# Emission order in place of the scheduler's on VectorE, ScalarE and GpSimd, in a loop of seven products per weight block

## The chip, the cores and the metric

The kernel runs on one core of one Trainium2 chip. The metric is the device time of one execution in microseconds, the median of several runs. Before the change it is 1908.83 us (three runs, 1908.06 to 1911.45).

## What is computed

The reference is a decoder trunk of two layers on 512 tokens of width 1024, all in float32. Each layer has two half-step SwiGLU blocks around a mixer (a gated short convolution in layer 0, differential attention in layer 1). Cut to the part that matters here, a SwiGLU block is

```python
def swiglu(x, w_gu, w_down):
    gate, up = jnp.split(x @ w_gu, 2, axis=-1)
    return (jax.nn.silu(gate) * up) @ w_down

h = h + 0.5 * rmsnorm(swiglu(rmsnorm(h, g[0]), ffn_w_gu[l, 0], ffn_w_down[l, 0]), g[1])
```

with 2816 hidden columns, and it runs four times: twice in each layer.

## The kernel before

**Precision.** Every float32 operand of a product is split into a high part `hi` (ScalarE writes it rounded to the matmul's float32r) and the rest `lo` (the operand minus `hi`, on VectorE or GpSimd). A product of two operands is three matmuls: hi by hi, hi by lo, lo by hi.

**The gate and up projection.** `ffn` works through 22 blocks `f` of 128 hidden columns. For the first four (`PLAIN`) function `job` multiplies directly. For the other 18, function `seven` treats the block as a 2 by 2 matrix of pieces (gate or up, by first or second half of the 1024 inputs: a11, a12, a21, a22) against a 2 by 2 matrix of token pieces (input half by left or right 256 tokens), and computes it with seven products of pieces instead of eight. The left factors are a11, a12, a22 themselves and four sums: s2 = a21 + a22 - a11, s1 = a21 + a22, s3 = a11 - a21, s4 = a12 - s2. The right factors are made once per FFN (`RightFactors`).

Each product is 12 matmuls of 128 by 128 by 256 columns (four tiles along the inputs, three matmuls each; function `product`, L336). They accumulate in three PSUM tiles a, b and c. The order of the products on TensorE, in the source, is: a11 into a, s2 into b, s1 into c, s3 into b, a12 into a, s4 into c, a22 into b. Between them the results are read out while the accumulation goes on:

- after a11, ScalarE copies a into u1 (L613); after s2, VectorE adds b and u1 to u2 (L598, `after6`)
- after s3, `after7`: VectorE makes u3 = b + u1 (L601) and, from it, su = c + u3 (L602)
- after a12, ScalarE takes the Silu of a (L617)
- after s4, `after3`: VectorE makes g2 = c + u2 (L605), and ScalarE its Silu (L606)
- after a22, `after4`: VectorE makes the last quarter su = b + u1 (L609), and GpSimd multiplies gate by up into `praw` (L611).

Since s4 goes on accumulating in c, its first matmul must wait until L602 has read c.

**The weights.** Class `Sum` makes the left factors of a later block while TensorE works on this one. There are eight buffers `wf`; when a product is closed, its buffer is free and the next factor in line is made, that of the product eight places later. A plain factor takes a ScalarE copy (L206) and a GpSimd subtraction (L207). A sum is formed in a PSUM tile `sums` by VectorE (L214 and L215 for s2 with s1 in passing, L221 for s3, L225 for s4), then ScalarE writes `hi` (L227), and VectorE writes `lo` (L229). That last step is held back in the source (`Sum.pending`, `flush`) until the next factor is made, so that VectorE does not sit waiting for ScalarE. L214 and L221 have two operands in SBUF, and the GpSimd operations L207 and L611 as well.

**What sets the order.** Nothing in the kernel orders the engines' queues by hand, apart from one short block at the start. Each engine runs its queue strictly in order, and a scheduler in the framework decides at build time what stands where. Two loads of 1 MB raw weights (`raw`, SyncE's queue) are in flight or in use at a time.

After the 22 blocks, `down` multiplies by the down projection (L384), again split in three matmuls.

Of the kernel before, what the change touches and what calls it, by code (L numbers as in the profile page):

```python
# [12 lines left out]
I32 = mybir.dt.int32  # L13
AF = mybir.ActivationFunctionType
ALU = mybir.AluOpType
PSUM = bass.MemoryType.PSUM
DRAM = bass.MemoryType.DRAM

# [5 lines left out]
NF = 2816 // P  # L24
# [8 lines left out]
PLAIN = 4  # L33
# [80 lines left out]
def trunk(ctx, tc, x, gu, dn, norm_g, cin, ck, cout, kvg, wk, wv, wq, lamp, subg, wo, out):  # L114
# [7 lines left out]
    work = ctx.enter_context(tc.tile_pool(name="work", bufs=1))  # L122
    psum = ctx.enter_context(tc.tile_pool(name="psum", bufs=1, space=PSUM))
    dram = ctx.enter_context(tc.tile_pool(name="dram", bufs=1, space=DRAM))
# [3 lines left out]
    def acc_tile(name):  # L128
        return psum.tile([P, 2, 512], F32, tag="acc", bufs=3, name=name)
# [30 lines left out]
    class Unit:  # L160
# [6 lines left out]
        def make(self):  # L167
# [5 lines left out]
            else:  # L173
# [5 lines left out]
                for a, (hi, lo) in enumerate(self.halves):  # L179
                    nc.vector.tensor_tensor(lo, raw[:, a * 512:(a + 1) * 512], hi.bitcast(F32), ALU.subtract)  # L180
            if self.u:
# [5 lines left out]
    class Sum:  # L187
# [10 lines left out]
        def make(self):  # L198
# [6 lines left out]
            if plain is not None:  # L205
                nc.scalar.activation(hi, plain, AF.Copy)  # L206
                nc.gpsimd.tensor_tensor(lo, plain, hi.bitcast(F32), ALU.subtract)  # L207
                Sum.flush()
            else:
# [3 lines left out]
                if self.form == "s2":  # L213
                    nc.vector.tensor_tensor(s0, a21, a22, ALU.add)  # L214
                    nc.vector.tensor_tensor(s1, s0, a11, ALU.subtract)  # L215
                    src = s1
                elif self.form == "s1":
                    src = s0
                elif self.form == "s3":
                    Sum.flush()  # L220
                    nc.vector.tensor_tensor(s0, a11, a21, ALU.subtract)  # L221
                    src = s0
                else:
                    Sum.flush()
                    nc.vector.tensor_tensor(s1, a12, s1, ALU.subtract)  # L225
                    src = s1
# [86 lines left out]
    def proj(o, key, u, xk, cols, ks=range(KT)):  # L313

        w = weights.get(key, u)
        n = cols.stop - cols.start
        for k in ks:
            hi, lo = w[k // 4]
            c = slice(k % 4 * P, (k % 4 + 1) * P)
            xh, xl = xk(k)  # L320
            for a, b in ((hi, xh), (hi, xl), (lo, xh)):
                nc.tensor.matmul(o[:, cols], a[:, c], b[:, cols],  # L322
                                 start=(k == 0 and b is xh and a is hi), stop=(k == KT - 1 and a is lo))
            later.tick(3 * 0.21 * n / 512)

    def close(*key):
        weights.done(*key)

    def product(o, key, xk, first, last):

        hi, lo = weights.get(*key)[0]
        for k in range(4):
            c = slice(k * P, (k + 1) * P)
            xh, xl = xk(k)
            for a, b in ((hi, xh), (hi, xl), (lo, xh)):
                nc.tensor.matmul(o, a[:, c], b, start=(first and k == 0 and b is xh and a is hi),  # L336
                                 stop=(last and k == 3 and a is lo), skip_group_check=True)
            later.tick(3 * 0.21 * 256 / 512)

    def two_then_two(nf, tail, stag):  # L340

        seq = [(f, t) for f in range(nf - tail) for t in range(NT)]
        for g in ((0, 1), (2, 3)):
            seq += [(f, t) for f in range(nf - tail, nf - stag) for t in g]
            for t in g:
                seq += [(f, t) for f in range(nf - stag, nf)] + [(None, t)]
        return seq
# [82 lines left out]
    def bcast(row, tag):  # L430
        g = work.tile([P, D], F32, tag=tag, bufs=1, name=tag)
        nc.sync.dma_start(g, row.partition_broadcast(P))
        return g
# [59 lines left out]
    def xk_of(xT):  # L493
        return lambda k: (xT[0][:, k, :], xT[1][:, k, :])

    def raw_blocks(pool):

        blocks = {}

        def place(f):  # L500
            if f // KT not in blocks:
                blocks[f // KT] = pool.tile([P, KT, S], F32, tag="praw", bufs=3, name="praw")
            return blocks[f // KT][:, f % KT, :]
        return place

    def raw_parts(pool, praws):
        def parts(f, toks):
            a, n = toks[0] * P, len(toks) * P
            ps = pool.tile([P, 2, S], F32R, tag="pair", bufs=3, name="psp")
            split(ps[:, 0, :n], ps[:, 1, :n], praws[f][:, a:a + n])  # L510

            def at(t):
                c = slice(t * P - a, (t + 1) * P - a)
                return ps[:, 0, c], ps[:, 1, c]
            return at
        return parts
# [44 lines left out]
    def ffn(pool, l, i, xT, finish, halves=True, right=None):  # L561
        key = f"{l}{i}"
        praws = [None] * NF
        place = raw_blocks(pool)
        tiles = {}

        def job(f, cols):
            if f not in tiles:
                tiles[f] = acc_tile("gu")
            ps = tiles[f]  # L570
            for s in range(2):
                proj(ps[:, s, :], "gu" + key, 2 * f + s, xk_of(xT), cols)
                if cols.stop == S:
                    close("gu" + key, 2 * f + s)
            if cols.stop == S:
                sil = pool.tile([P, 2, S], F32, tag="pair", bufs=3, name="sil")[:, 0, :]
                nc.scalar.activation(sil, ps[:, 0, :], AF.Silu)
                praws[f] = place(f)
                nc.vector.tensor_tensor(praws[f], sil, ps[:, 1, :], ALU.mult)

        def seven(f, e):

            if e == 0:
                tiles["abc"] = [acc_tile(n) for n in "abc"]
            a, b, c = (t[:, e, LEFT] for t in tiles["abc"])
            tmp = work.tile([P, 4, 256], F32, tag="tmp", bufs=2, name="u")
            u1, u2, u3, g2 = (tmp[:, n, :] for n in range(4))
            su = pool.tile([P, 2, S], F32, tag="pair", bufs=3, name="su")

            def step(o, form, factor, first, last, then):  # L590
                product(o, ("gu" + key, f, form), right.t[factor], first, last)
                then()
                if f == NF - 1 and factor in right.slots:
                    right.done(factor)
                close("gu" + key, f, form)

            def after6():
                nc.vector.tensor_tensor(u2, b, u1, ALU.add)  # L598

            def after7():  # L600
                nc.vector.tensor_tensor(u3, b, u1, ALU.add)  # L601
                nc.vector.tensor_tensor(su[:, 1, RIGHT], c, u3, ALU.add)  # L602

            def after3():
                nc.vector.tensor_tensor(g2, c, u2, ALU.add)  # L605
                nc.scalar.activation(su[:, 0, RIGHT], g2, AF.Silu)  # L606

            def after4():
                nc.vector.tensor_tensor(su[:, 1, LEFT], b, u1, ALU.add)  # L609
                praws[f] = place(f)  # L610
                nc.gpsimd.tensor_tensor(praws[f], su[:, 0, :], su[:, 1, :], ALU.mult)  # L611

            step(a, "a11", "b11", True, True, lambda: nc.scalar.activation(u1, a, AF.Copy))  # L613
            step(b, "s2", "t2", True, True, after6)
            step(c, "s1", "t1", True, True, lambda: None)
            step(b, "s3", "t3", False, True, after7)
            step(a, "a12", "b21", False, True, lambda: nc.scalar.activation(su[:, 0, LEFT], a, AF.Silu))  # L617
            step(c, "s4", "b22", False, True, after3)
            step(b, "a22", "t4", False, True, after4)

        if halves:
            later.keep(2)
            for f in range(3):
                job(f, FIRST)
            later.keep(0)
            right = RightFactors(pool, xT)
        for f in range(PLAIN):
            job(f, SECOND if halves and f < 3 else ALL)
            if f == 1:
                right.one_three()  # L630
            if f == 2:
                right.two()
        right.four()
        for f in range(PLAIN, NF):
            seven(f, (f - PLAIN) % 2)
        g_post = bcast(norm_g[l, 1 if i == 0 else 5], "gpost")
        st = finish()
        down("dn" + key, two_then_two(NF, TAIL, STAG), raw_parts(pool, praws), lambda t, y: st(t, y, g_post, True))
# [401 lines left out]
```

## Time and profile before

| | |
|---|---|
| median of three runs | 1908.83 us (1908.06 to 1911.45) |
| the profiled execution, its own time | 1910.82 us |
| its span, first to last instruction | 1907.8 us |
| TensorE busy | 98% of the span |
| VectorE, ScalarE, GpSimd busy | 58%, 43%, 28% |
| mean granted TensorE clock | 0.998 |

The four stretches in which `seven` runs take some 187.5 us each, 750 us in all. A page of the profile and the answers drawn from its trace count times in microseconds from the first instruction, and name an instruction by its source line, its output and its inputs; "L336 PE c" is a matmul of line 336 that writes tile c. Matmuls are pipelined: the end of the last one of a product lies some 0.16 us after the next product's first one has started, and so a busy TensorE can still be a delayed one. What counts is when the next product starts.

### The profile page before, as it was taken

The numbers are of one execution on the slowest core, as the hardware profiler recorded it, in microseconds if no ns is written. First come the engines' busy times: TensorE is split into PE (matmuls) and PEld (weight loads), VectorE is DVE, ScalarE is ACT, GpSimd is POOL, SyncE is SP. The second block draws the span as 40 slices with busy tenths as digits, with TensorE's granted clock in tenths as the row PEclk, the third lists the DMA queues.
The fourth block names the chain that finished last, engine by engine and source line by source line (L and its number), as shares of the span: only waits on it lengthen the run. The fifth ranks groups of instructions, "written<-read, shape, count | busy, mean of one in ns | idle before, by whom it ended". The sixth has DMA issues, their size and how long they took to land. (4 is left out here: it accounts for less than half of the span.)

```text
span 1907.8 us, 29851 instructions
## 1 busy us (share of the span) xinstructions
PE 1861.6 (98%) x11968; PEld 1677.9 (88%) x11968; DVE 1109.1 (58%) x1837; ACT 828.9 (43%) x1566; POOL 528.2 (28%) x538
## 2 busy tenths in 40 slices
PE   7999999999999999999999999999999999999998
PEld 7999988888889999988878999988886789999886
DVE  6766653554456666633654666653668467676533
ACT  4444443432244454532533454542457434544422
POOL 3354510100014554300230455500114233545100
PEclk9999999999999999999999999999999999999999
DMA  5232342142321322421443223243232022323421
GB/s 194 87 104 96 111 142 101 58 142 90 109 78 57 110 99 101 155 90 66 142 167 122 89 89 111 92 152 111 102 117 87 28 78 89 101 99 111 142 80 44
DMA packets 41546, 197.67 MB, mean 104 GB/s; under 512 B 3648, under 2 KB 8000, under 8 KB 27584
## 3 DMA queue, kind: packets, MB, share of 16 engines
q1 hardware_dynamic: 39616, 189.49, 29.0%
q0 software_dynamic: 1792, 6.29, 0.8%
q8 instruction: 93, 1.52, 0.3%
q14 instruction: 45, 0.37, 0.1%
HBM read 187.38 MB, written 8.39 MB: 103 GB/s over the span
## 5 line engine op out<-in xcount | busy, mean ns | idle before, releaser
L207 POOL TENSOR_TENSOR wf<-raw,wf 128x512 fp32r<-128x512 f32 x216 | 294.2, 1374 | 440.3 <-ACT wf L206 440.3
L384 PE MATMUL y<-wf,psp 128*128 128x512 f32 x1344 | 310.2, 389 | 0.0
L384 PEld LDWEIGHTS y<-wf,psp 128*128 128x128 f32 x1344 | 251.8, 188 | 51.9
L227 ACT ACTIVATE wf<-sums 128x512 fp32r<-128x512 f32 x288 | 171.8, 597 | 253.2 <-PE b L336 182.5
L229 DVE TENSOR_TENSOR wf<-sums,wf 128x512 fp32r<-128x512 f32 x288 | 192.4, 689 | 100.5 <-ACT wf L227 82.4
L180 DVE TENSOR_TENSOR wf<-raw,wf 128x512 fp32r<-128x512 f32 x214 | 148.6, 708 | 175.1 <-ACT wf L178 174.5
L442 POOL TENSOR_SCALAR rb<-ss 128x1 f32<-128x1 f32 x84 | 26.7, 317 | 794.4 <-ACT junk L439 788.4
L178 ACT ACTIVATE wf<-raw 128x512 fp32r<-128x512 f32 x214 | 131.1, 626 | 243.3 <-PE y L384 126.2
L336 PE MATMUL b<-wt,wf 128*128 128x256 f32 x1728 | 230.8, 283 | 0.0
L336 PE MATMUL a<-x_hi,wf 128*128 128x256 f32 x1152 | 230.8, 283 | 0.0
L384 PE MATMUL y<-wt,psp 128*128 128x512 f32 x960 | 222.6, 389 | 0.0
L336 PEld LDWEIGHTS b<-wt,wf 128*128 128x128 f32 x1728 | 217.7, 192 | 0.0
L384 PEld LDWEIGHTS y<-wt,psp 128*128 128x128 f32 x960 | 179.9, 188 | 37.2
L336 PEld LDWEIGHTS a<-x_hi,wf 128*128 128x128 f32 x1152 | 190.1, 192 | 0.2
L206 ACT ACTIVATE wf<-raw 128x512 fp32r<-128x512 f32 x216 | 136.1, 630 | 69.0 <-PE c L336 37.7
L336 PE MATMUL a<-x_lo,wf 128*128 128x256 f32 x576 | 163.0, 283 | 0.0
L462 DVE TENSOR_TENSOR psp<-praw,psp 128x512 fp32r<-128x512 f32 (+1 forms) x126 | 69.9, 561 | 124.6 <-ACT psp L461 124.6
L461 ACT ACTIVATE psp<-praw 128x512 fp32r<-128x512 f32 (+1 forms) x126 | 65.4, 523 | 167.2 <-PE y L384 166.8
L462 DVE TENSOR_TENSOR wt<-raw,wt 128x1024 fp32r<-128x1024 f32 x77 | 95.7, 1250 | 63.6 <-ACT wt L461 63.5
L336 PE MATMUL c<-x_hi,wf 128*128 128x256 f32 x576 | 121.7, 295 | 7.8 <-DVE su L602 2.1
L336 PE MATMUL b<-x_hi,wf 128*128 128x256 f32 x576 | 118.3, 283 | 0.0
L336 PE MATMUL c<-wt,wf 128*128 128x256 f32 x864 | 115.4, 283 | 0.0
(157 smaller groups left out, 3396.8 us busy)
## 6 DMA issues: line engine op xcount, KB each, us to landing
raw<-gu SPq DMA_DIRECT2D x88, 1024.0 KB, 4.8
raw<-dn SPq DMA_DIRECT2D x44, 1024.0 KB, 4.9
raw<-cin SPq DMA_DIRECT2D x12, 1024.0 KB, 4.7
raw<-cout SPq DMA_DIRECT2D x4, 1024.0 KB, 4.8
raw<-wk SPq DMA_DIRECT2D x4, 1024.0 KB, 4.8
raw<-wv SPq DMA_DIRECT2D x4, 1024.0 KB, 5.9
kscr<-kk POOLq DMA_DIRECT2D x8, 512.0 KB, 6.7
raw<-wq SPq DMA_DIRECT2D x4, 1024.0 KB, 4.9
```

The costliest lines, as they stand in the source:

```text
L178: nc.scalar.activation(hi, raw[:, a * 512:(a + 1) * 512], AF.Copy)
L180: nc.vector.tensor_tensor(lo, raw[:, a * 512:(a + 1) * 512], hi.bitcast(F32), ALU.subtract)
L206: nc.scalar.activation(hi, plain, AF.Copy)
L207: nc.gpsimd.tensor_tensor(lo, plain, hi.bitcast(F32), ALU.subtract)
L227: nc.scalar.activation(hi, src, AF.Copy)
L229: Sum.pending.append((self, lambda: nc.vector.tensor_tensor(lo, src, hi.bitcast(F32), ALU.subtract)))
L336: nc.tensor.matmul(o, a[:, c], b, start=(first and k == 0 and b is xh and a is hi), stop=(last and k == 3 and a is lo), skip_group_check=True)
L384: nc.tensor.matmul(y[t][:, c, :], a, w[c][b], start=(f == first[t] and a is ph and b == 0), stop=(f == last[t] and a is pl))
L442: nc.gpsimd.tensor_scalar(b, ss, m / n, m * EPS, ALU.mult, ALU.add)
L461: nc.scalar.activation(hi, src, AF.Copy)
L462: nc.vector.tensor_tensor(lo, src, hi.bitcast(F32), ALU.subtract)
```

## The change

The loop over the 18 blocks is put into a block in which the three named engines keep the order in which the kernel emits their work. TensorE and SyncE stay with the scheduler. The set of instructions, their shapes and the tiles stay the same on every engine. Line numbers in the changed file are higher by one up to the loop, and by two behind it.

```diff
+ET = mybir.EngineType
...
-        for f in range(PLAIN, NF):
-            seven(f, (f - PLAIN) % 2)
+        with tc.manual_schedule(engines={ET.DVE, ET.Activation, ET.Pool}):
+            for f in range(PLAIN, NF):
+                seven(f, (f - PLAIN) % 2)
```

What moves is the same in every block, in all four FFNs. The first place is VectorE (DVE), one block in the steady part of the loop. Before:

```order
L221 TENSOR_TENSOR sums<-raw 128x512
L601 TENSOR_TENSOR u<-b,u 128x256
L229 TENSOR_TENSOR wf<-sums,wf 128x512
L602 TENSOR_TENSOR su<-c,u 128x256
L225 TENSOR_TENSOR sums<-raw,sums 128x512
L229 TENSOR_TENSOR wf<-sums,wf 128x512
L605 TENSOR_TENSOR u<-c,u 128x256
L214 TENSOR_TENSOR sums<-raw 128x512
L609 TENSOR_TENSOR su<-b,u 128x256
L215 TENSOR_TENSOR sums<-sums,raw 128x512
```

The same block after the change:

```order
L222 TENSOR_TENSOR sums<-raw 128x512
L602 TENSOR_TENSOR u<-b,u 128x256
L603 TENSOR_TENSOR su<-c,u 128x256
L230 TENSOR_TENSOR wf<-sums,wf 128x512
L226 TENSOR_TENSOR sums<-raw,sums 128x512
L606 TENSOR_TENSOR u<-c,u 128x256
L230 TENSOR_TENSOR wf<-sums,wf 128x512
L610 TENSOR_TENSOR su<-b,u 128x256
L215 TENSOR_TENSOR sums<-raw 128x512
L216 TENSOR_TENSOR sums<-sums,raw 128x512
```

Three exchanges: the read of c (L602 before, L603 now) stands ahead of the `lo` of s3; the read of c after s4 (L605, now L606) ahead of the `lo` of s4; and the read of b after a22 (L609, now L610) ahead of the first sum of a later block (L214, now L215).

On ScalarE (ACT) one instruction moves: the second Silu (`su<-u`), ahead of the copy of a22. From the Silu of a on, before:

```order
L617 ACTIVATE su<-a 128x256
L227 ACTIVATE wf<-sums 128x512
L206 ACTIVATE wf<-raw 128x512
L606 ACTIVATE su<-u 128x256
L206 ACTIVATE wf<-raw 128x512
```

and after the change:

```order
L618 ACTIVATE su<-a 128x256
L228 ACTIVATE wf<-sums 128x512
L607 ACTIVATE su<-u 128x256
L207 ACTIVATE wf<-raw 128x512 x2
L614 ACTIVATE u<-a 128x256
```

So the copies of a22 and of the next a11 (`wf<-raw`) now stand both behind that Silu. On GpSimd the product L611 moves in the same way from behind the `lo` of the next block's a11 to ahead of it: L207 for a22, then L611, then L207 for a11. On TensorE the scheduler has changed one thing by itself. From the last matmuls of a12 (tile a) on, before:

```order
L336 MATMUL a<-x_lo,wf 128x256
L336 MATMUL a<-x_hi,wf 128x256
L336 MATMUL b<-x_hi,wf 128x256
L336 MATMUL b<-x_lo,wf 128x256
L336 MATMUL c<-x_hi,wf 128x256
L336 MATMUL c<-x_lo,wf 128x256
```

and after the change:

```order
L337 MATMUL a<-x_lo,wf 128x256
L337 MATMUL a<-x_hi,wf 128x256
L337 MATMUL c<-x_hi,wf 128x256
L337 MATMUL c<-x_lo,wf 128x256
L337 MATMUL c<-x_hi,wf 128x256 x2
```

The first two matmuls of a22 (tile b), which stood ahead of s4 (tile c) in 17 of the 18 blocks of each FFN, now follow it like the other ten. SyncE's queue is the same.

## Rows read from the trace of the kernel before

**Rows 1.** The page: the span, and each engine's busy time and share.
```profile
span 1907.8 us, 29851 instructions
PE 1861.6 (98%) x11968; PEld 1677.9 (88%) x11968; DVE 1109.1 (58%) x1837; ACT 828.9 (43%) x1566; POOL 528.2 (28%) x538
```

**Rows 2.** Windows, the four loops: stretch, length, busy us of each engine, clock, DMA.
```profile
65.40:253.10 187.70, 185.61 (x1512) 182.13 (x1511) 128.19 (x234) 94.46 (x183) 90.99 (x68) 1.00 0.31 107
607.10:794.60 187.50, 185.62 (x1512) 182.14 (x1511) 128.20 (x234) 94.40 (x183) 90.99 (x68) 1.00 0.31 107
1059.40:1246.90 187.50, 185.60 (x1513) 182.15 (x1512) 128.18 (x234) 94.31 (x183) 91.05 (x68) 1.00 0.32 107
1591.80:1779.30 187.50, 185.61 (x1513) 182.15 (x1512) 128.20 (x234) 94.36 (x183) 90.94 (x68) 1.00 0.32 107
```

**Rows 3.** Chain that ended last: start, length, what; one block, then the last.
```profile
1634.01 1.44 PE a L336 x12
...
1744.05 0.61 ACT wf L227
1744.68 0.69 DVE wf L229
1745.37 0.34 DVE su L602
1745.75 1.70 PE c L336 x12
...
1769.49 1.44 PE a L336 x12
...
1775.25 1.44 PE a L336 x12
1776.69 1.44 PE c L336 x12
...
1779.57 119.72 PE y L384 x528
```

**Rows 4.** Timeline of TensorE: start, length, instruction; the s3 product of one block.
```profile
1638.16 1.60 PE L336 MATMUL b<-wt,wf 128*128 128x256 f32 x12
```

**Rows 5.** Timeline of VectorE in and behind it; in brackets idle time before.
```profile
1639.80 0.42 DVE L601 TENSOR_TENSOR u<-b,u 128x256 f32<-128x256 f32 x1
1640.45 0.69 DVE L229 TENSOR_TENSOR wf<-sums,wf 128x512 fp32r<-128x512 f32 x1 [0.23 <-ACT wf L227]
1641.06 0.41 DVE L602 TENSOR_TENSOR su<-c,u 128x256 f32<-128x256 f32 x1
...
1643.74 0.69 DVE L214 TENSOR_TENSOR sums<-raw 128x512 f32<-128x512 f32 x1
...
1648.10 1.29 DVE L229 TENSOR_TENSOR wf<-sums,wf 128x512 fp32r<-128x512 f32 x2 [0.27 <-POOL praw L611]
```

**Rows 6.** Timeline of ScalarE in the same block.
```profile
1643.32 0.63 ACT L206 ACTIVATE wf<-raw 128x512 fp32r<-128x512 f32 x1 [0.55 <-PE c L336]
...
1645.96 0.38 ACT L613 ACTIVATE u<-a 128x256 f32<-128x256 f32 x1 [0.82 <-PE a L336]
1646.24 0.59 ACT L227 ACTIVATE wf<-sums 128x512 fp32r<-128x512 f32 x1
```

**Rows 7.** Timeline of GpSimd in the same block.
```profile
1644.03 2.80 POOL L207 TENSOR_TENSOR wf<-raw,wf 128x512 fp32r<-128x512 f32 x2 [1.73 <-ACT wf L206]
```

**Rows 8.** Timeline of GpSimd behind the first loop.
```profile
254.00 1.29 POOL L611 TENSOR_TENSOR praw<-su 128x512 f32<-128x512 f32 x1 [8.08 <-DVE su L609]
```

**Rows 9.** Timeline of VectorE at the same time.
```profile
254.10 1.75 DVE L180 TENSOR_TENSOR wf<-raw,wf 128x512 fp32r<-128x512 f32 x1 [0.24 <-ACT wf L178]
```

**Rows 10.** Groups on VectorE: busy us, mean ns of one, idle before and releaser.
```profile
L542 DVE TENSOR_TENSOR t<-xr 128x1024 f32<-128x1024 f32 x4 | 13.6, 3402 | 14.3 <-POOL xr L528 14.3
...
L545 DVE TENSOR_TENSOR t<-xr 128x1024 f32<-128x1024 f32 x4 | 4.9, 1222 | 6.9 <-POOL xr L528 6.9
```

## The prediction

> **What bounds the kernel now.** I read the page first: TensorE is busy for 98% of the span, no other engine for more than 58% [rows 1]. So there is at most a little to be had on TensorE, and it sits where a busy TensorE is held up without looking idle. The windows of the four loops come next: each takes some 187.5 us at full clock, and TensorE counts as busy for all but 2 us of it [rows 2]. The third view is the chain that ended last, where the loss shows [rows 3]. In every block but the last the chain leaves TensorE once: ScalarE's `hi` (0.61 us), VectorE's `lo` (0.69 us), then L602, the read of c, and only then the s4 product into c, whose 12 matmuls are drawn out to 1.70 us where the others take 1.44. From the a11 at 1634.01 to the one at 1769.49 lie 13 blocks, 10.42 us each. In the last block of the loop no sum is left to be made, nothing stands between L601 and L602, and the chain stays on TensorE: a12 1.44, s4 1.44, and from 1769.49 to 1779.57 only 10.08 us. That is 7 products of 1.44 us, nothing lost. So **0.34 us per block** hang on L602.
>
> The timelines show why L602 is late. The s3 product starts at 1638.16 and takes 1.60 us to its last result [rows 4], so it is done at 1639.76, and VectorE's L601 begins 0.04 us later [rows 5]. It ends at 1640.22. The next instruction in VectorE's queue is the `lo` of s3 of the following block, which waits for ScalarE's `hi` (0.23 us idle) and then runs 0.69 us. L602 starts at 1641.06 and ends at 1641.47 [rows 5]. The a12 product, the only thing ahead of s4 apart from two matmuls of a22, has issued its last matmul by 1641.04.
>
> **The change part by part.** Nothing is added or removed; 0 us there.
>
> *L602 ahead of the `lo` of s3.* L602 can start when L601 ends, at about 1640.25, and is done at about 1640.66. TensorE is ready for s4 after s3 and a12, at 1638.16 + 2 x 1.44 = 1641.04, some 0.38 us later. The wait is gone: 0.34 us in each of the 17 blocks of a loop that have it, four loops: 17 x 4 x 0.34 = **23.1 us**. Against the windows [rows 2]: they sum to 750.2 us, 72 blocks of 10.08 us are 725.8, so 24.4 us lie above the floor; the 1.3 us more are a few longer blocks, which I leave in, since I do not see that the order makes them. Both ends: 0 if L602 is not what holds s4, and 24.4 if the longer blocks go too.
>
> *The two matmuls of a22 behind s4.* Same work in another place; they filled 0.24 us (two twelfths of 1.44) of a wait that is no longer there. 0 us.
>
> *The `lo` of s3 behind L602, and L605 ahead of the `lo` of s4.* L605 makes VectorE wait for the end of s4, and the `lo` of s4 waits behind it. That weight belongs to the next block, some 8 us on. 0 us; what covers it is a block's lead of eight buffers.
>
> *L606 ahead of the copies, L609 ahead of L214, L611 ahead of L207 of a11.* Here a cover could go, since these three make one loop with the wait just removed. I count it from the first matmul of s4, by rows: s4 1.60 [rows 4]; L605, as L602, 0.41 [rows 5]; L606, shape of L613, which gives up ScalarE after 0.28; the copy L206 of a22 0.63 [rows 6]; its L207 on GpSimd 1.29, the length of an L611 of the same shape [rows 8]. Now the sum: L214 has two operands in SBUF, and so has L180, which began 0.10 us after that L611 and took 1.75 us, against 0.69 for this shape [rows 5, 9]: it ended 0.56 us after GpSimd did. In the old order L214 started first (1643.74, against 1644.03 for L207 [rows 5, 7]) and was not held up. In the new one it stands behind L609, which needs the end of a22, and L207 comes first; so I add 0.56 us for L214 behind L207. Then L215, as L214, 0.69 [rows 5]; two L227 of 0.59 [rows 6]; two L229 1.29; L221, as L214, 0.69; L601 0.42; L602 0.41 [rows 5]. Sum: 1.60 + 0.41 + 0.28 + 0.63 + 1.29 + 0.56 + 0.69 + 1.18 + 1.29 + 0.69 + 0.42 + 0.41 = 9.45 us. The hand-overs between engines are 0.02 to 0.08 us each (ACT to DVE 1744.66 to 1744.68, DVE to PE 1745.71 to 1745.75 [rows 3], ACT to POOL 1643.95 to 1644.03 [rows 6, 7]); for ten of them I take 0.5 us. The loop closes in some **9.95 us, against 10.08 us** that TensorE needs for a block. It fits, with 0.1 us to spare; where L214 does not have to wait, with some 0.4. So I cost it at 0 us, and keep the narrow margin for the range: each 0.1 us by which the sum is short beyond the margin costs 6.8 us over 68 blocks.
>
> The Trainium skill (SBUF — State Buffer, section "Who interferes with whom") says that a VectorE instruction with two SBUF inputs and a GpSimd instruction that reads SBUF exclude each other, and that the first holds the shared port to its end. The L180 agrees in kind (1.75 us); by the rule's letter L214 would run its full 0.69 us after L207 in place of 0.56, the loop would close in 10.08 us, and the gain would still stand, just.
>
> *Other waits.* L611 now holds GpSimd ahead of a11's L207, 1.3 us; that factor is needed a block later, 0 us. The raw loads hang on the last L207 of a block, which moves by less than 1 us against some 10 us of lead; 0 us. SyncE's queue is unchanged.
>
> **Sum.** The profiled execution took 1910.82 us around a span of 1907.8, and lies 2.0 us above the median. 1910.82 - 23.1 = 1887.7 us for it, and for the median **1908.83 - 23.1 = 1885.7 us**, 1.2% less.
>
> **The rivals.**
>
> *A part of the wait stays.* If the loop above closes later than 10.08 us, the remainder comes back at s4 in every block. For it: the margin is 0.1 us on a sum of twelve durations, and L214 will be held back by a GpSimd instruction. Against it: the rows err by some hundredths each. With the loop 0.25 us longer than I think, 0.12 us x 68 = 8 us stay: 1894 us.
>
> *GpSimd keeps its place over two instructions: slower.* In the new order GpSimd has L207, L611 and L207 in its queue while L214 waits. If L214 got through only after L611 as well, 1.29 us more, the loop would close in 11.24 us, 1.16 above TensorE's 10.08 and 0.82 above today's block: 68 x 0.82 = 56 us slower, 1964 us. It turns from gain to loss when L214 loses more than about 0.13 + 0.34 = 0.47 us beyond my count. Against it: L542, with two SBUF operands, fell among four GpSimd instructions on the same data, and took 3.40 us against 1.22 for L545 of the same shape [rows 10]: 2.2 us lost, about one of those GpSimd instructions and not several. L180's 1.75 us likewise. On this the same page of the Trainium skill says that whichever issues first holds the port; it does not say who comes next.
>
> *Nothing changes.* If the profile names the wrong releaser, and s4 in truth waits for its own weights or a buffer, it stays at 1909 us. Against it: the last block, with L601 and L602 adjacent already, has no wait [rows 3], and the order shows that the exchange is made in every block.
>
> **How the numbers follow.** Forecast 1885.7 us: 0.72; its own range is 1882 to 1889, from 24.4 us of gain and some 2 us by which executions differ (1908.06 to 1911.45) up to 20 us of gain. A part stays: 0.17, 1889 to 1900. No change: 0.05. Slower by GpSimd: 0.06. The range of 8 in 10 takes in the forecast and the larger half of the second case: 1881.5 to 1896. What a measurement can tell from no change is 0.2%, 3.8 us. Faster: 0.72 + 0.17 = 0.89; the same: 0.05; slower: 0.06.
>
> **What would show it.** Right: blocks of 10.08 us in the chain, without ScalarE and VectorE between; the four windows 181.5 to 182 us each; the wait of PE c for L602 gone from the list of waits; L214 at some 1.5 us in place of 0.69, L207 of a22 at 1.29 in place of 1.5 (2.80 for the two [rows 7]), and L611 longer by some 0.4. Wrong: PE c still drawn out, now behind L221 and L601 that start late (the narrow margin); L214 at 2.5 us or more (the slower rival); or s4 waiting with L602 long done (the wrong releaser).

## The result and the profile after

The changed kernel takes **1884.78 us** (median of four runs, 1883.7 to 1887.16) against 1908.44 us for the kernel before in the same comparison: ratio 0.9875, 95% interval 0.9863 to 0.9887, or 23.7 us less. The forecast was 1885.7 us. In a second set of runs the changed kernel took 1883.41 us (ratio 0.9864, 0.9849 to 0.9878).

The page of the changed kernel, span and engines, against [rows 1]:

```profile
span 1881.8 us, 29723 instructions
...
PE 1843.7 (98%) x11968; PEld 1673.5 (89%) x11968; DVE 1172.3 (62%) x1837; ACT 825.8 (44%) x1566; POOL 540.4 (29%) x538
```

The span is 26.0 us shorter, yet TensorE's busy share still reads 98%: the busy time fell with the span, by 17.9 us, because most of the time lost before had been counted as busy. VectorE is busy 63 us longer with the same 1837 instructions. Some 54 us of that are one line, L215, waiting inside the instruction, as the timelines below show; most of the rest is that neighbouring instructions overlap less.

The windows of the four loops (stretch, length, busy us of PE, PEld, DVE, ACT and POOL, clock, DMA), against [rows 2]:

```profile
64.10:245.70 181.60, 181.60 (x1513) 181.42 (x1512) 144.05 (x233) 93.03 (x181) 93.98 (x68) 1.00 0.32 111
599.90:781.40 181.50, 181.50 (x1513) 181.41 (x1513) 144.26 (x233) 92.98 (x182) 94.02 (x68) 1.00 0.33 111
1045.90:1227.30 181.40, 181.40 (x1512) 181.33 (x1511) 144.04 (x233) 93.02 (x181) 94.02 (x68) 1.00 0.33 111
1571.90:1753.30 181.40, 181.40 (x1512) 181.33 (x1511) 144.04 (x233) 93.02 (x181) 94.01 (x68) 1.00 0.33 111
```

They sum to 725.9 us against 750.2 before: 24.3 us, nearly the whole change. Of the rest of the span's 26.0 us, 1.3 lie ahead of the first loop, which starts at 64.1 us in place of 65.4, before any instruction that the change moves; in the other kernels below that start lies anywhere from 64.3 to 66.7.

The chain that ended last, one block of the last loop (start, length, what), against [rows 3]:

```profile
1632.55 1.44 PE a L337 x12
1633.99 1.44 PE b L337 x12
...
1638.31 1.44 PE a L337 x12
1639.75 1.44 PE c L337 x12
...
1642.63 0.48 PE a L337 x4
```

From a11 to a11, 1632.55 to 1642.63, is 10.08 us. ScalarE and VectorE are gone from the chain. All blocks of the four loops take 10.08 us but one of 10.25 and the last of each loop (10.17): the loop stands at TensorE's floor.

The 1.70 us that the old chain shows for the s4 product must not be set against 1.44. The chain counts a product that follows without a pause from the end of the one before it, and one that had to wait from its own first matmul; counted that way, an undisturbed product takes 1.60 us [rows 4]. TensorE's timeline shows where the 0.34 us of a block were. Before, the first three matmuls around the start of s4 (tile c):

```profile
1641.16 0.28 PE L336 MATMUL b<-x_lo,wf 128*128 128x256 f32 x1
1641.53 0.39 PE L336 MATMUL c<-x_hi,wf 128*128 128x256 f32 x1
1641.76 0.28 PE L336 MATMUL c<-x_lo,wf 128*128 128x256 f32 x1
```

and after:

```profile
1639.47 0.28 PE L337 MATMUL a<-x_hi,wf 128*128 128x256 f32 x1
1639.59 0.28 PE L337 MATMUL c<-x_hi,wf 128*128 128x256 f32 x1
1639.71 0.28 PE L337 MATMUL c<-x_lo,wf 128*128 128x256 f32 x1
```

Matmuls that do not wait start 0.12 us apart. Before, s4 started 0.37 us after the matmul ahead of it, so 0.25 us late, and its own first matmul was longer (0.39 us in place of 0.28), which cost some 0.10 us more. In all 68 blocks that have this wait that first matmul takes 0.38 to 0.39 us, and so does the first matmul of the products that wait in experiments 1, 2, 4, 9 and 11; the rows do not say why.

VectorE in the same place (start, length, instruction; in brackets idle time before it and what ended it), against [rows 5]:

```profile
1638.43 0.42 DVE L602 TENSOR_TENSOR u<-b,u 128x256 f32<-128x256 f32 x1
1638.89 0.42 DVE L603 TENSOR_TENSOR su<-c,u 128x256 f32<-128x256 f32 x1
1639.27 0.69 DVE L230 TENSOR_TENSOR wf<-sums,wf 128x512 fp32r<-128x512 f32 x1
...
1642.67 0.42 DVE L610 TENSOR_TENSOR su<-b,u 128x256 f32<-128x256 f32 x1 [0.42 <-PE b L337]
1643.01 1.55 DVE L215 TENSOR_TENSOR sums<-raw 128x512 f32<-128x512 f32 x1
1644.60 0.70 DVE L216 TENSOR_TENSOR sums<-sums,raw 128x512 f32<-128x512 f32 x1
```

and GpSimd, against [rows 7]:

```profile
1642.71 1.30 POOL L208 TENSOR_TENSOR wf<-raw,wf 128x512 fp32r<-128x512 f32 x1 [1.58 <-ACT wf L207]
1643.96 1.75 POOL L612 TENSOR_TENSOR praw<-su 128x512 f32<-128x512 f32 x1
1645.68 1.29 POOL L208 TENSOR_TENSOR wf<-raw,wf 128x512 fp32r<-128x512 f32 x1
```

L603, the read of c, ends at 1639.31, 0.28 us before s4 starts (1639.59). Before, s4 started 0.06 us after that read (L602 ended at 1641.47 [rows 5]), so some 0.22 us are to spare. L215 (the old L214) starts 0.30 us after GpSimd's L208 and takes 1.55 us in place of 0.69. It ends at 1644.56, 0.55 us after L208 does, and then it is L612's turn to be drawn out: it starts before L215 is through and takes 1.75 us where 1.30 is its length alone.

Below, lines go by the changed file, one above those of the kernel before; **exchange 1, 2 and 3** are the three on VectorE: the read of c (L603) ahead of the `lo` of s3; the read of c after s4 (L606) ahead of the `lo` of s4; the read of b (L610) ahead of the first sum (L215).

### The profile page after: what moved, and what is told of

It reads as the page before. It is cut to its first block, busy times and chain, and to the rows that moved or that the text cites. A ratio compares the mean times of both kernels' runs of the same rounds, so it can differ in the third digit from the quotient of the medians.

```text
span 1881.8 us, 29723 instructions
## 1 busy us (share of the span) xinstructions
PE 1843.7 (98%) x11968; PEld 1673.5 (89%) x11968; DVE 1172.3 (62%) x1837; ACT 825.8 (44%) x1566; POOL 540.4 (29%) x538
## 5 line engine op out<-in xcount | busy, mean ns | idle before, releaser
L208 POOL TENSOR_TENSOR wf<-raw,wf 128x512 fp32r<-128x512 f32 x216 | 282.0, 1305 | 402.0 <-ACT wf L207 402.0
L228 ACT ACTIVATE wf<-sums 128x512 fp32r<-128x512 f32 x288 | 164.9, 596 | 275.5 <-DVE sums L222 149.9
L207 ACT ACTIVATE wf<-raw 128x512 fp32r<-128x512 f32 x216 | 134.9, 624 | 21.4 <-PE gu L323 11.2
L462 ACT ACTIVATE psp<-praw 128x512 fp32r<-128x512 f32 (+1 forms) x126 | 65.4, 523 | 165.7 <-PE y L385 165.4
L612 POOL TENSOR_TENSOR praw<-su 128x512 f32<-128x512 f32 x72 | 122.5, 1702 | 32.6 <-DVE su L610 32.6
L337 PE MATMUL c<-x_hi,wf 128*128 128x256 f32 x576 | 115.5, 283 | 0.0
```

The source lines that it names most:

```text
L228: nc.scalar.activation(hi, src, AF.Copy)
L462: nc.scalar.activation(hi, src, AF.Copy)
```

## The experiments

**1. Exchange 1 by hand, the rest left to the scheduler.** The theory was that the read of c alone carries the gain.

```diff
-            step(b, "s3", "t3", False, True, after7)
+            with tc.manual_schedule(engines={ET.DVE}):
+                step(b, "s3", "t3", False, True, after7)
```

> Only the s3 step of each block keeps the emission order, and only on VectorE: L602 stands ahead of the lo of s3, everything else stays as the scheduler has it (L214 ahead of the read of b after a22, ScalarE and GpSimd as before). Theory (the place of L602 is the whole gain): blocks of 10.08 us, 1883 to 1888 us, the same as the changed kernel within 0.2%. Rival (the other exchanges, or the three engines together, carry part of it): clearly above, 1890 to 1909 us. Beside it, L214 should run 0.69 us again and not be held up by GpSimd.

Measured: 1897.02 us (1895.62 to 1901.31), ratio 0.9944 (0.9929 to 0.9959). A miss: only half of the gain. (The scheduler, given this start, made exchange 2 as well, not 3.) The blocks alternate between 10.08 and 10.50 us. The chain of such a longer block shows who took L603's place:

```profile
1634.73 1.46 PE c L337 x12
...
1636.21 0.09 DVE u L606
...
1636.55 0.69 DVE wf L230
...
1637.27 1.56 DVE sums L215
1638.83 0.34 DVE su L610
...
1639.21 1.70 PE b L337 x12
```

L215 is held for 1.56 us, the read of b (L610) stands behind it, and s2 of the next block, which writes b, starts late. That is so in every second block only. In the source a tile b serves two blocks, one in each half. The s2 that writes the second half starts 0.06 us after the read of the first half has ended (1639.15 to 1639.21); the s2 after it, which begins a new tile, starts at 1649.39, while the read of b (1649.24 to 1649.65) still runs. Whether the first of these waits is needed at all, the two halves being different memory, was not tried. GpSimd's timeline in the same block:

```profile
1636.98 2.98 POOL L208 TENSOR_TENSOR wf<-raw,wf 128x512 fp32r<-128x512 f32 x2 [1.14 <-ACT wf L207]
```

L208 came 0.29 us ahead of L215. In the kernel before it was the other way round: VectorE at 1643.74 [rows 5], GpSimd at 1644.03 [rows 7].

**2. The order kept on ScalarE and GpSimd alone.**

```diff
-        with tc.manual_schedule(engines={ET.DVE, ET.Activation, ET.Pool}):
+        with tc.manual_schedule(engines={ET.Activation, ET.Pool}):
```

> ScalarE and GpSimd keep the emission order, VectorE goes back to the scheduler's (L602 behind the lo of s3). Theory: the wait for L602 is back in every block, 10.42 us, 1905 to 1912 us. Rival (the order on ScalarE and GpSimd matters): below 1900 us.

Measured: 1910.94 us (1908.39 to 1911.81), ratio 1.0010 (1.0001 to 1.0019). The list of waits has TensorE waiting for the read of c again (five waits, 2.1 us in all, as in the kernel before; the short wait of every block is not in that list), and the blocks take 10.42 us. These two engines' order gives nothing by itself.

**3. The order kept on VectorE alone** (`engines={ET.DVE}`).

> VectorE alone keeps the emission order, ScalarE and GpSimd go back to the scheduler's. Theory: 10.08 us a block, 1883 to 1888 us. The copy of a22 stands ahead of the second Silu again, so L207 of a22 starts some 0.3 to 0.5 us earlier and holds L214 up for less: L214 at 1.0 to 1.3 us in place of 1.55. Rival (the three engines must go together): above 1890 us.

Measured: 1884.45 us (1882.29 to 1887.63), ratio 0.9875 (0.9858 to 0.9891): all of the gain. The time came as expected, the length of L215 did not: 0.84 us in the median. VectorE's order here differs from experiment 1 in exchange 3 alone; that pair is worth 12.6 us once exchange 1 is made. (GpSimd's order differs too: the scheduler has now put the product L612 ahead of a11's L208, as the change does. The L208 that holds L215 is that of a22, and it stands first in both.)

**4. The loop made too long.** In the changed kernel the `lo` of s3 is put between L602 and the read of c; the other exchanges stay.

```diff
                 nc.vector.tensor_tensor(u3, b, u1, ALU.add)
+                Sum.flush()
                 nc.vector.tensor_tensor(su[:, 1, RIGHT], c, u3, ALU.add)
```

> All as in the changed kernel, but the lo of s3 is put out ahead of the read of c again. If the place of L602 alone counts, this is the kernel before: 10.42 us a block, 1908 us. If the loop through GpSimd counts (s4, L605, Silu, copy of a22, L207, L214 held up, L215, L227 twice, L229 twice, L221), L221 now ends later than before, and hi, lo and L602 follow it: the loop closes in some 10.8 us, 0.4 above the kernel before, 1925 to 1945 us.

Measured: 1941.55 us (1941.07 to 1944.92), ratio 1.0177 (1.0162 to 1.0193). A hit. Here the chain runs round the loop that the prediction summed (L604 is the read of c; the lines from there on are one higher):

```profile
1702.94 1.70 PE c L337 x12
...
1706.22 1.80 DVE sums L215
1708.04 0.71 DVE sums L216
...
1710.03 1.30 DVE wf L230 x2
1711.35 0.71 DVE sums L222
...
1712.16 0.61 ACT wf L228
...
1712.80 0.69 DVE wf L230
1713.48 0.34 DVE su L604
...
1713.87 1.70 PE c L337 x12
```

1702.94 to 1713.87 is 10.93 us per block, 0.85 above TensorE's 10.08. The loop exists, and it sets the time when it does not fit.

**5 and 6. One and three extra copies on ScalarE**, of 128 by 256, behind the second Silu of the changed kernel, to eat up the margin from GpSimd's side.

```diff
                 nc.scalar.activation(su[:, 0, RIGHT], g2, AF.Silu)
+                pad = work.tile([P, D], BF16, tag="junk", bufs=1, name="pad")
+                for _ in range(1):
+                    nc.scalar.activation(pad[:, :256], g2, AF.Copy)
```

> The changed kernel with one more ScalarE copy of 128x256, used by nobody, behind the second Silu, that is inside the loop from s4 back to s4; it holds ScalarE for 0.28 to 0.4 us. In the changed kernel L602 ends 0.28 us before s4 starts, of which 0.05 is the hand-over, so the loop has some 0.1 to 0.2 us to spare. Theory: the rest, 0.05 to 0.3 us a block, shows at s4: 1888 to 1905 us. Rival (the margin is only idle time and not closed in a loop): 1884 to 1886 us.

> The same with three copies, 0.85 to 1.2 us of ScalarE. Theory: 0.65 to 1.05 us a block at s4, 68 blocks, 1929 to 1956 us, and the chain runs through L606, ScalarE, L207, L214 and L221. Rival (no loop): 1884 to 1886 us.

Measured: 1885.24 us (1883.49 to 1886.38) and 1888.85 us (1887.02 to 1889.67); ratios 0.9871 (0.9855 to 0.9888) and 0.9891 (0.9876 to 0.9905). Both missed, the second by 40 us, and no block in the loop grew: all stay at 10.08 us, with 0.3 and 1.1 us more once per loop. VectorE and GpSimd with one copy:

```profile
1634.66 0.69 DVE L215 TENSOR_TENSOR sums<-raw 128x512 f32<-128x512 f32 x1
```

```profile
1634.66 1.84 POOL L208 TENSOR_TENSOR wf<-raw,wf 128x512 fp32r<-128x512 f32 x1 [2.17 <-ACT wf L207]
```

and with three (L613 is the read of b):

```profile
1636.02 0.42 DVE L613 TENSOR_TENSOR su<-b,u 128x256 f32<-128x256 f32 x1 [0.41 <-PE b L337]
1636.36 0.69 DVE L215 TENSOR_TENSOR sums<-raw 128x512 f32<-128x512 f32 x1
```

```profile
1637.27 1.30 POOL L208 TENSOR_TENSOR wf<-raw,wf 128x512 fp32r<-128x512 f32 x1 [3.12 <-ACT wf L207]
```

The copies delay ScalarE's L207 and with it L208, so L215 comes first and runs 0.69 us: with one copy by less than 0.01 us, in all 64 blocks in which the two meet, and L208 is the one held (1.84 us); with three, L215 is done before GpSimd starts. The delay meant to lengthen the loop took 0.86 us of hold out of it.

**7. The changed kernel again**, beside 5 and 6.

> The changed kernel again, on the same chip as the two with copies, to compare with: 1883 to 1888 us.

Measured: 1883.41 us (1882.76 to 1884.37), as told above.

**8. Experiment 1 with the emitted order on ScalarE and GpSimd too.** Exchange 3 is still not made.

```diff
-            step(b, "s3", "t3", False, True, after7)
+            with tc.manual_schedule(engines={ET.DVE}):
+                step(b, "s3", "t3", False, True, after7)
...
-        for f in range(PLAIN, NF):
-            seven(f, (f - PLAIN) % 2)
+        with tc.manual_schedule(engines={ET.Activation, ET.Pool}):
+            for f in range(PLAIN, NF):
+                seven(f, (f - PLAIN) % 2)
```

> As the kernel in which only the s3 step keeps its order on VectorE (1897 us), and besides ScalarE and GpSimd keep the emission order throughout the loop; VectorE still has L214 ahead of the read of b. There, L207 of a22 began 0.3 us before L214 and held it up (1.56 us), and the read of b and with it the next s2 came late in every second block. Theory (it is the shared access of GpSimd and VectorE, and who comes first): the copy of a22 now stands behind the Silu, which waits for L605, so L207 starts some 0.4 us behind L214; L214 runs 0.69 us, L207 is the one held up, the read of b is on time, and the loop is at 10.08 us a block: 1883 to 1888 us. Rival (L214 ahead of the read of b is late by itself): 1897 us again.

Measured: 1884.76 us (1882.85 to 1885.65), ratio 0.9873 (0.9857 to 0.9889): a hit. ScalarE's second Silu ahead of L207 makes L208 later; L215 starts at 1633.14 and L208 at 1633.56, the hold is gone, and the read of b behind L215 is in time. So there are two ways to cure what experiment 1 laid bare: take the read of b out from behind the held instruction, or let that instruction come first.

**9 and 10. One and three extra VectorE instructions** of 128 by 256 between L215 and L216 of the changed kernel: inside the loop, but behind the place where VectorE and GpSimd meet.

```diff
                     nc.vector.tensor_tensor(s0, a21, a22, ALU.add)
+                    for _ in range(1):
+                        nc.vector.tensor_tensor(s1[:, :256], s0[:, :256], a11[:, :256], ALU.subtract)
                     nc.vector.tensor_tensor(s1, s0, a11, ALU.subtract)
```

> The changed kernel with one more VectorE operation of 128x256 between L214 and L215 (0.34 to 0.45 us), so behind the point where GpSimd can be overtaken. L602 ends 0.28 us ahead of s4 in the changed kernel, 0.05 of it hand-over. Theory (the loop from s4 back to s4 closes with 0.1 to 0.2 us to spare): 0.1 to 0.35 us a block, 68 blocks, 1891 to 1908 us. Rival (the loop has much more room than counted): 1883 to 1887 us.

> The same with three such operations (1.0 to 1.35 us). Theory: 0.8 to 1.2 us a block, 1938 to 1966 us, 0.68 to 0.9 us a block more than with one. Rival: below 1920 us.

Measured with one: 1905.4 us (1903.73 to 1907.41), ratio 0.9981 (0.9971 to 0.9992), a hit. The block takes 10.42 us, 0.34 more, for an instruction that takes 0.46 in the row. Of the 0.34, some 0.10 are s4's first matmul, which takes 0.39 us again now that s4 has to wait; so s4 is 0.24 us late, and 0.22 us were to spare, the figure found above. With three: 1891.34 us (1889.36 to 1892.15), ratio 0.9907 (0.9893 to 0.9922). A miss: three cost 14 us less than one. VectorE and GpSimd with three, in the first two such blocks of the last loop (a shortened view; lines behind L215 are two higher):

```profile
1587.73 1.55 DVE L215 TENSOR_TENSOR sums<-raw 128x512 f32<-128x512 f32 x1
...
1598.72 0.69 DVE L215 TENSOR_TENSOR sums<-raw 128x512 f32<-128x512 f32 x1
```

```profile
1587.43 1.30 POOL L208 TENSOR_TENSOR wf<-raw,wf 128x512 fp32r<-128x512 f32 x1 [1.85 <-ACT wf L207]
...
1598.78 1.78 POOL L208 TENSOR_TENSOR wf<-raw,wf 128x512 fp32r<-128x512 f32 x1 [1.45 <-ACT wf L207]
```

The first L215 is held, and the block takes 10.99 us (1587.73 to 1598.72). After that one stall VectorE comes 0.06 us ahead of GpSimd and stays ahead: 0.86 us less of hold pays for much of the 1.4 us that were added, and the blocks that follow take 10.08 to 10.13 us but for one of 10.41, one of 10.24 and the last of each loop. With one extra instruction L208 stays some 0.3 us ahead of L215, and the stall recurs in every block.

**11. Exchange 1 alone.** In experiment 1, L606 (which waits for s4) stood ahead of the `lo` of s4; was it that which made L215 late?

```diff
-            step(b, "s3", "t3", False, True, after7)
-            step(a, "a12", "b21", False, True, lambda: nc.scalar.activation(su[:, 0, LEFT], a, AF.Silu))
-            step(c, "s4", "b22", False, True, after3)
+            with tc.manual_schedule(engines={ET.DVE}):
+                step(b, "s3", "t3", False, True, after7)
+                step(a, "a12", "b21", False, True, lambda: nc.scalar.activation(su[:, 0, LEFT], a, AF.Silu))
+                Sum.flush()
+                step(c, "s4", "b22", False, True, after3)
```

> VectorE keeps the emitted order only at step s3 and the steps behind it up to s4, so that L602 and L603 come first as in the change, but the lower part of s4's stage stands ahead of L605 and L214 ahead of L609, as in the kernel before. Theory (L609 need stand ahead of L214 only because L605, which waits for the end of s4, has been put ahead of that lower part and so makes L214 later than GpSimd's L207): here L214 starts about 0.5 us after the end of s4 and ahead of L207 at about 0.8 us, takes 0.69 us, b is read in time, blocks of 10.08 us, 1883 to 1888 us. Rival (L609's place is needed however early L214 starts): the read of b is late in about every second block, near 1897 us, as with step s3 alone.

Measured: 1897.64 us (1896.74 to 1898.17), ratio 0.9941 (0.9924 to 0.9957). The theory falls, the rival holds. VectorE and GpSimd:

```profile
1633.24 0.41 DVE L606 TENSOR_TENSOR u<-c,u 128x256 f32<-128x256 f32 x1
1633.57 1.63 DVE L215 TENSOR_TENSOR sums<-raw 128x512 f32<-128x512 f32 x1
1635.12 0.41 DVE L610 TENSOR_TENSOR su<-b,u 128x256 f32<-128x256 f32 x1
```

```profile
1633.35 2.99 POOL L208 TENSOR_TENSOR wf<-raw,wf 128x512 fp32r<-128x512 f32 x2 [1.14 <-ACT wf L207]
```

L215 is behind again, by 0.22 us. The expectation had carried over its old distance from s4, and that was the error. From L226, the sum of s4, to L215 VectorE takes 2.35 us here (1631.22 to 1633.57) as before (L225 at 1641.39 to 1643.74). But before, s4 waited for the read of c, which stands right ahead of that sum in the queue, so the sum began 0.14 us ahead of s4's first matmul (1641.53); here s4 no longer waits and starts at 1630.94, 0.28 us ahead of the sum. GpSimd's L208 moves with TensorE, since its buffer is set free by s4: 2.50 us behind s4's first matmul before, 2.41 here. **The wait that exchange 1 takes away had been giving VectorE its lead over GpSimd.**

**12. Exchanges 1 and 3 without 2**, on VectorE alone.

```diff
-        with tc.manual_schedule(engines={ET.DVE, ET.Activation, ET.Pool}):
+        with tc.manual_schedule(engines={ET.DVE}):
...
+            Sum.flush()
             step(c, "s4", "b22", False, True, after3)
```

> VectorE keeps the emitted order in the whole loop, but the lower part of s4's stage is put back ahead of L605, as in the kernel before: exchanges 1 and 3 without exchange 2. The run with exchange 1 alone (near 1897 us) has shown that the place of L605 is not what makes L214 late. Theory (exchange 2 costs and gives nothing, exchange 3 is what keeps the read of b out of L214's hold): blocks of 10.08 us, L214 held at about 1.55 us behind L609, 1883 to 1888 us. Rival (the three belong together: with L605 later, its successor on ScalarE and GpSimd's product come later, and the hold of L214 pushes the next block): some blocks above 10.08 us, 1890 us or more.

Measured: 1882.27 us (1881.47 to 1883.31), ratio 0.9863 (0.9847 to 0.9879); every block takes 10.08 us. The time is the theory's (its range missed by 0.7 us at the lower end); the hold is shorter than it said. VectorE and GpSimd:

```profile
1640.61 0.42 DVE L610 TENSOR_TENSOR su<-b,u 128x256 f32<-128x256 f32 x1 [0.36 <-PE b L337]
1640.96 0.84 DVE L215 TENSOR_TENSOR sums<-raw 128x512 f32<-128x512 f32 x1
```

```profile
1639.94 1.30 POOL L208 TENSOR_TENSOR wf<-raw,wf 128x512 fp32r<-128x512 f32 x1 [1.14 <-ACT wf L207]
1641.20 1.75 POOL L612 TENSOR_TENSOR praw<-su 128x512 f32<-128x512 f32 x1
```

L208 starts 1.02 us ahead of L215 and ends at 1641.24; L215 ends at 1641.80, 0.56 us later, as in the changed kernel. With ScalarE's copy where the scheduler had it, L208 is early, and 0.71 us of the hold go. Exchange 2 gives nothing. The median lies below the changed kernel's 1884.78 and 1883.41, but the intervals of the ratios overlap, and the loops cannot be shorter than 10.08 us a block: not a version that can be called faster.

Together (the hold is L215's length, 0.69 to 0.70 us when free):

| kernel | exchanges on VectorE | ScalarE, GpSimd | L215, us | block, us | time, us |
|---|---|---|---|---|---|
| before | none | scheduler's | 0.69 | 10.42 | 1908.4 |
| 11 | 1 | scheduler's | 1.63 | 10.08 and 10.50 | 1897.6 |
| 1 | 1, 2 | scheduler's | 1.56 | 10.08 and 10.50 | 1897.0 |
| 12 | 1, 3 | scheduler's* | 0.84 | 10.08 | 1882.3 |
| 3 | 1, 2, 3 | scheduler's* | 0.84 | 10.08 | 1884.5 |
| 8 | 1, 2 | as emitted | 0.70 | 10.08 | 1884.8 |
| after | 1, 2, 3 | as emitted | 1.55 | 10.08 | 1884.8 |

(* with L612 ahead of a11's L208, as in the changed kernel.) Exchange 3 without exchange 1 was not tried.

## Why the prediction was right, and where it was incomplete

**The term of the sum.** 23.1 us were forecast for L602's place, with 24.4 as the upper end if the 1.3 us of a few longer blocks went too. The loops gave 24.3 and the median 23.7. So the 1.3 us belonged into the term: the five longer blocks hung on the read of c as well (the list of waits of the kernel before has five waits of s4 for L602, 2.1 us in all). In four of them VectorE paused ahead of a pair of `lo`, in the last loop at 1616.84 (L229, 0.62 us idle in place of the usual 0.27 [rows 5]), and L602 and s4 came 0.35 us later; in the fifth ScalarE paused ahead of a `hi` (L227 at 217.86, 2.52 us idle in place of 2.24). Experiment 12 has pauses of that size on VectorE in the same four blocks, and none of its blocks grows; in the changed kernel one pause of 0.29 us is left, and it makes the one block of 10.25 (0.29 less the 0.22 to spare, and 0.10 for the first matmul). What the pause itself is remains open.

**The cause of the wait.** Right: with the read of c moved, s4's wait left the list of waits and the chain; with the order kept on the other two engines only, it came back (experiment 2).

**The step that was incomplete** is the one on L609 ahead of L214, which was costed at 0 us as a place "where a cover could go". It is where more than half of the gain comes from: exchange 1 alone gives 10.6 us (experiment 11), exchanges 1 and 3 give 26.4 (experiment 12). The prediction asked what happens to L214 in the new order and found that it would be held; it did not ask what would be late next in the old order with L602 moved. There L214 is held as well, and the read of b stands behind it. The sum came out right because the change makes both exchanges.

**The narrow margin.** Forecast 9.95 us for the loop, 0.13 to spare; measured 9.86, 0.22 to spare, by the rows of the changed kernel and by experiment 9 alike. The sum was 0.09 us too long, mainly because neighbours on one engine overlap by some 0.1 us (the two L228 take 1.08 us together in place of 1.18; L602 starts 0.60 us behind L222 in place of 0.69). The added 0.56 us for L214 behind L207 measured 0.55 and 0.56 (1.55 us in all, where "some 1.5" was forecast; L612 at 1.75 against 1.30, "longer by some 0.4"). By the rule of the Trainium skill (SBUF — State Buffer, "Who interferes with whom"), read to the letter, the blocked instruction runs in full afterwards; the rows give 0.55 and 0.56 us in place of 0.69. With the 0.13 us of difference the loop would close in 9.99 us and still fit.

**"Each 0.1 us beyond the margin costs 6.8 us"** is too low even for a delay behind L214 that is too short to change who comes first, since it leaves out the 0.10 us that a wait costs on top: in experiment 9 the loop was 0.24 us too long, 16 us by the rule, and 21 were measured (1905.4 less 1884.8; 0.34 us in 64 blocks are 22). It fails for a delay ahead of GpSimd's L207 (experiments 5 and 6) and for one long enough to turn the order round (experiment 10). In these runs the loop keeps to one of two courses, L214 held or L214 free, and a larger delay can throw it into the one that is free. The rival "a part stays" took for granted that only the first exists.

**The slower rival** fell as argued: VectorE gets in between two GpSimd instructions that are queued back to back (L215 ends at 1644.56, while L612, started at 1643.96, waits its turn). **The rival of no change** fell with the chain.

## What to carry to other kernels

When a wait is taken off the critical path, go through each queue again with the later engine now early: the wait may have been what kept two other engines out of each other's way, and the next instruction in line behind the new hold may be the next read that a product needs. On an engine that works in order, put the reads that free an accumulator ahead of work whose result is needed a block later, and above all ahead of work that another engine can hold. A margin measured by adding work is only good for the place where the work was added, and what the wait itself costs (0.10 us here) must be taken off first.

## What the runs showed that was not expected

- Who starts first between VectorE's L215 and GpSimd's L208 decides between 0.69 and 1.55 us, and less than 0.01 us is enough to be first (experiment 5, with the same outcome in all 64 blocks). The loser pays: L208 took 1.84 us there, 1.78 in experiment 10, 1.42 in experiment 8, 1.30 alone. It does not pay its full length: L215 ends 0.55 to 0.56 us after the L208 that held it (0.69 alone), and L612 1.15 us after the L215 that held it (1.30 alone).
- More work can take less time: three extra VectorE instructions per block gave 1891.3 us, one gave 1905.4.
- A product that waits for its accumulator can hide in a busy share of 98%: the sign is the start of its first matmul, 0.37 us after the one before it in place of 0.12, and that matmul's length, 0.39 us in place of 0.28.
